# A hybrid decoder layer on one core: first loads in one block, one power for four norms, two turnings of the queue moved, last rows in smaller pieces

## Chip, cores and metric

The kernel runs on 1 core of one Trainium2 chip, in float32. The metric is device time in microseconds (us), the median of several executions; a profile is taken from one execution.

## What is computed

One layer over 512 tokens of width 1024 (reference, cut):

```python
h  = rmsnorm(x, g_mix);  z = h @ w_in           # 1024 x 9728: all projections
rq, rk, rv, rg, aq, ak, av, gl = split(z)
# A: retention, 4 heads, chunks of 128, rotated q and k, decay, group norm, swish gate
# B: 3 groups of 4 heads, dilated causal attention (window, step) = (128,1), (512,4), (2048,16),
#    q and k rms-normed and rotated; the groups merged by their softmax denominators
x  = x + (sig(g_A) * (A @ W_A) + sig(g_B) * (B @ W_B)) @ w_o
x  = x + square(relu(rmsnorm(x) @ w_up)) @ w_down
x  = x + sig(rmsnorm(x) @ w_ple_gate) * (p @ w_ple_proj)
```

## The kernel before

Every large matmul runs in three passes over split operands: each float32 operand is cut into a high part (`hi`) and a low part (`lo`), and `mm3` adds hi*hi, hi*lo and lo*hi. Weights come from HBM in units of 256 rows x 512 columns (512 KB, `raw`), ScalarE (ACT) makes the high part `whi` and VectorE (DVE) the low part `wlo` (`split_unit`, L237 and L238). A plan lists all units in their order; `fetch(n)` issues loads on SyncE's queue (SP) up to unit n, `ahead(n)` splits units ahead of use.

`setup` loads the transposed x (`x_cols`, 8 chunks of 128 rows) and the first panel of `w_in` (group 0's q, 4 units) in alternating transfers of 256 KB on SP; the first chunk of weights comes in two halves of 64 partitions, one on ACT's queue, one on SP's. `first_panel` splits x and weights chunk by chunk in a fixed order and begins with chunk 0: hi*hi, lo*hi, hi*lo for four tiles of 128 tokens (L468, L470, L472), then chunks 1 to 3, then for each token tile chunks 4 to 7. `load_tables` and `fetch(6)` (two more units) follow the first loads, then four tiles of x (512 KB each) whose squares `token_squares` takes.

The q projection of group 0 is not normed at once: the tokens' factors come late. For the first three tiles `consume` only takes sums of squares and rotates. At the last tile it takes the tokens' squares, `token_factors` (power on POOL, L527), then four times `factor` (a DVE instruction and a power of 128x4 on POOL, L613 and L614) and four times `scale` (a DVE multiplication of 128x512, L618). In group 0's q and k ACT and DVE keep the written order (`manual_schedule`); elsewhere a list scheduler orders each engine's instructions by readiness and by their order of emission.

TensorE's order around the small stages comes from a queue: `later(lag, fn)` puts a step behind `lag` ticks, a tick comes after every six large matmuls or so, and at every second tick up to two ready steps are emitted, the first in the list first:

```python
def tick(self):
    self.clock += 1
    if self.clock % self.PACE:
        return
    for _ in range(self.PACE):
        i = next((i for i, (ready, _, _) in enumerate(self.queue) if ready <= self.clock), None)
```

So transposes and attention steps stand between the matmuls of the next projection. `merge` is such a step (12 ticks after the last attention group's projections): it computes the merge weights on DVE into `wide` (cw), turns them on TensorE (pc, L756), copies the result (ct), writes it to DRAM (c_dram) and later reads it back broadcast, one row of 512 per head and group (`load`, cb, first three 4 ticks later), multiplies and adds (`weigh`, first 8 ticks later; each step also issues a load three items on). `heads_T` turns rotated heads (ph, L559): four transposes of 128x128 per head, after `lag` ticks. `ret_proj` projects and rotates the retention keys and calls it with 9; after it follow the projections of v and of the gate, then the retention heads that read the turned keys.

At the end `fin` computes sigmoid (ACT), product and sum (DVE) of an output tile and stores it; the last token tile of the second half is made in two column halves of 256.

Of the kernel before, what the change touches and what calls it, by code (L numbers as in the profile page):

```python
# [11 lines left out]
F32 = mybir.dt.float32  # L12
# [64 lines left out]
class Block:  # L77
# [299 lines left out]
    def setup(self):  # L377
        nc, a = self.nc, self.a
        self.gcol = self.const.tile([P, 48], F32, name="gcol")
        xr = [self.big("xr") for _ in range(2)]  # L380
        self.x_cols = [xr[k // 4][:, k % 4] for k in range(KD)]
        nc.scalar.dma_start(self.gcol, a["vec_cols"])
        for u in range(KD // 2):
            src, _ = self.plan[u]
            raw = self.wraw.tile([P, 1024], F32, tag="raw", name=self.nm("raw")).rearrange("p (k n) -> p k n", k=2)
            for k in range(2):
                c = slice((2 * u + k) * P, (2 * u + k + 1) * P)
                nc.sync.dma_start(self.x_cols[2 * u + k], a["x_cols"][c])
                w = src[k * P : (k + 1) * P]
                if u or k:  # L390
                    nc.sync.dma_start(raw[:, k], w)
                else:
                    nc.scalar.dma_start(raw[: P // 2, k], w[: P // 2])
                    nc.sync.dma_start(raw[P // 2 :, k], w[P // 2 :])
            self.raws.append((raw, None))
        self.load_tables()
        self.fetch(6)
        self.x_tiles = []
# [181 lines left out]
    def att_proj(self, g, n):  # L580
# [5 lines left out]
        def consume(t, ps):  # L586
# [8 lines left out]
            if not lazy:  # L595
                factor(t)
                if t:
                    scale(t - 1)
                if t == NT - 1:
                    scale(t)  # L600
            elif t == NT - 2:
                self.token_squares(0)
            elif t == NT - 1:
                self.token_squares(2)
                self.token_factors()
                for i in range(NT):
                    factor(i)
                for i in range(NT):
                    scale(i)
# [112 lines left out]
    def merge(self, groups, oh, ol):  # L722
# [30 lines left out]
        for g in range(NG):  # L753
            nc.vector.tensor_copy(wide[:, g * H * NT : (g + 1) * H * NT].rearrange("p (h r) -> p r h", h=H), cs[g])
        ps = self.bank("pc")
        nc.tensor.transpose(ps[: NG * H * NT, :P], wide, self.ident)  # L756
        turned = self.tmp("ct")[: NG * H * NT, :P]
        nc.scalar.activation(turned, ps[: NG * H * NT, :P], AF.Copy)
        cd = self.dram.tile([NG * H, S], F32, name="c_dram", tag="c_dram")
        nc.sync.dma_start(cd.rearrange("a (r l) -> (a r) l", r=DIL), turned)  # L760
        accs, spread = [None] * H, {}
# [22 lines left out]
        for i, (h, g) in enumerate(items):  # L784
            if i == 0:
                for p in items[:3]:
                    self.later(4, lambda p=p: load(*p))

            def step(i=i, h=h, g=g):
                weigh(h, g)  # L790
                if i + 3 < len(items):
                    load(*items[i + 3])
            self.later(8, step, ("O", h, g))


    def ret_proj(self, extra=None):
# [9 lines left out]
        self.rows_gemm(self.hT, KD, consume)  # L806
        return self.heads_T(rots, False, 9)

# [254 lines left out]
    def tail(self, mx):  # L1063
# [85 lines left out]
        for half in range(2):  # L1149
# [3 lines left out]
            def fin(t, ps, i=slice(0, 512)):  # L1153
                s, o = self.tmp("fs"), self.tmp("fo")
                c = slice(half * 512 + i.start, half * 512 + i.stop)
                nc.scalar.activation(s[:, i], ps[:, i], AF.Sigmoid, scale=r3[:, t : t + 1])
                nc.vector.tensor_tensor(o[:, i], s[:, i], pp[half][:, t, i], op=ALU.mult)
                nc.vector.tensor_tensor(s[:, i], o[:, i], xs[t][:, c], op=ALU.add)
                nc.sync.dma_start(out[t * P : (t + 1) * P, c], s[:, i])

# [65 lines left out]
```

## Time and profile before

| | |
|---|---|
| median of 3 runs | 996.74 us (996.7 to 998.17) |
| the profiled execution | 997.21 us, its span 995.4 us |
| TensorE busy | 984.7 us, 99% of the span |
| VectorE, ScalarE, GpSimd busy | 647.6, 461.8, 97.4 us |
| granted TensorE clock | full in all 40 slices |

The span is what the profiler saw from the first to the last instruction; the time also has what lies around it. TensorE's busy time is from modelled ends of matmuls: its matmuls of 512 columns start closer together than the duration shown. What it waits for is read from the rows below.

### The profile page before, as it was taken

How to read it: one execution, taken by the hardware profiler on the slowest of the kernel's cores; microseconds unless marked ns; L12 is line 12 of the kernel's file. 1: busy time of each engine (PE TensorE's matmuls, PEld its weight loads, DVE VectorE, ACT ScalarE, POOL GpSimd, SP SyncE). 2: the span in 40 equal slices, each digit the busy share in tenths (PEclk: the TensorE clock that was granted, in tenths of full speed). 3: DMA queues.
4: the chain of work that ended last, by engine and by line, in shares of the span. 5: the costliest groups of instructions: out<-in, count | busy, mean ns of one | idle time of the engine just before them, and what ended most of it. 6: DMA issues, size and time to landing. Idle time of an engine off the chain costs nothing.

```text
span 995.4 us, 12449 instructions
## 1 busy us (share of the span) xinstructions
PE 984.7 (99%) x4588; PEld 826.1 (83%) x4588; DVE 647.6 (65%) x1014; ACT 461.8 (46%) x938; POOL 97.4 (10%) x98
## 2 busy tenths in 40 slices
PE   8999999999999999999999999999999999999998
PEld 6788899889887888888888878888888888888886
DVE  6866675774878344554643696668667759766953
ACT  5535344433433334342422447764564565465451
POOL 0210220220000010001002010110101001000000
PEclk9999999999999999999999999999999999999999
DMA  9632132323353312222346496758659766875911
GB/s 337 240 101 76 54 106 85 105 76 106 93 142 120 113 43 85 86 85 85 132 146 166 125 233 193 190 128 225 179 136 212 203 167 153 238 160 131 312 54 53
DMA packets 90781, 141.15 MB, mean 142 GB/s; under 512 B 6320, under 2 KB 40416, under 8 KB 90720
## 3 DMA queue, kind: packets, MB, share of 16 engines
q1 hardware_dynamic: 79616, 119.22, 37.5%
q0 software_dynamic: 10880, 20.97, 12.7%
q8 instruction: 36, 0.59, 0.2%
q10 hardware_dynamic: 224, 0.16, 0.1%
q14 instruction: 25, 0.20, 0.1%
HBM read 136.10 MB, written 4.24 MB: 141 GB/s over the span
## 4 chain that ended last, share of the span: by engine, by line
PE 94%; DVE 4%; issue 1%; DMA 0%; ACT 0%; POOL 0%; ACTq 0%; DVEq 0%; POOLq 0%
PE pg L251 25%; PE pg L250 25%; PE pg L249 25%; PE pb L251 3%; PE pb L249 3%; PE pb L250 3%; PE po L700 1%; PE ph L559 1%; PE pt L325 1%; PE sc L677 1%; DVE wlo L238 1%; PE ry L899 1%; PE pe L651 1%; PE kv L887 1%; PE sc L683 1%
## 5 line engine op out<-in xcount | busy, mean ns | idle before, releaser
L238 DVE TENSOR_TENSOR wlo<-raw,whi 128x1024 fp32r<-128x1024 f32 (+1 forms) x166 | 196.8, 1191 | 103.8 <-ACT whi L237 101.8
L237 ACT ACTIVATE whi<-raw 128x1024 fp32r<-128x1024 f32 (+1 forms) x165 | 169.5, 1032 | 195.3 <-PE pg L251 75.4
L249 PE MATMUL pg<-whi,hh 128*128 128x512 f32 x444 | 178.6, 402 | 0.0
L250 PE MATMUL pg<-wlo,hh 128*128 128x512 f32 x444 | 173.6, 391 | 1.0 <-DVE wlo L238 1.0
L251 PE MATMUL pg<-whi,hl 128*128 128x512 f32 x444 | 173.7, 391 | 0.0
L250 PEld LDWEIGHTS pg<-wlo,hh 128*128 128x128 f32 x444 | 91.4, 206 | 15.3 <-DVE wlo L238 1.4
L251 PEld LDWEIGHTS pg<-whi,hl 128*128 128x128 f32 x444 | 91.1, 205 | 15.1
L249 PEld LDWEIGHTS pg<-whi,hh 128*128 128x128 f32 x444 | 91.3, 206 | 14.0
L249 PE MATMUL pg<-h2h,whi 128*128 128x512 f32 x256 | 99.6, 389 | 0.0
L250 PE MATMUL pg<-h2l,whi 128*128 128x512 f32 x256 | 99.6, 389 | 0.0
L251 PE MATMUL pg<-h2h,wlo 128*128 128x512 f32 x256 | 99.6, 389 | 0.0
L242 ACT ACTIVATE whi<-raw,gcol 128x256 fp32r<-128x256 f32 (+1 forms) x144 | 66.1, 523 | 21.3 <-PE pg L250 12.4
L243 DVE SCALAR_TENSOR_TENSOR wlo<-raw,gcol,whi 128x256 fp32r<-128x256 f32 (+1 forms) x144 | 65.5, 510 | 15.6 <-ACT whi L242 15.6
L202 POOL DMA_DIRECT2D raw<-in_w_down x32 | 38.6, 1206 | 302.4 <-DMA raw<-in_w_down 147.8
L249 PE MATMUL pg<-hh,whi 128*128 128x512 f32 x160 | 64.0, 400 | 0.0
L249 PE MATMUL pg<-whi,uh 128*128 128x512 f32 x160 | 62.8, 392 | 0.0
L251 PE MATMUL pg<-whi,ul 128*128 128x512 f32 x160 | 62.6, 392 | 0.0
L250 PE MATMUL pg<-wlo,uh 128*128 128x512 f32 x160 | 62.4, 390 | 0.0
L251 PE MATMUL pg<-hh,wlo 128*128 128x512 f32 x160 | 62.4, 390 | 0.0
L250 PE MATMUL pg<-hl,whi 128*128 128x512 f32 x160 | 62.3, 390 | 0.0
L250 PEld LDWEIGHTS pg<-h2l,whi 128*128 128x128 f32 x256 | 48.0, 188 | 10.0
L251 PEld LDWEIGHTS pg<-h2h,wlo 128*128 128x128 f32 x256 | 48.0, 188 | 10.0
(201 smaller groups left out, 1685.2 us busy)
## 6 DMA issues: line engine op xcount, KB each, us to landing
raw<-in_w_in SPq DMA_DIRECT2D x72, 512.0 KB, 4.1
raw<-in_w_down SPq DMA_DIRECT2D x48, 512.0 KB, 4.3
raw<-in_w_up SPq DMA_DIRECT2D x32, 512.0 KB, 5.2
raw<-in_w_down POOLq DMA_DIRECT2D x32, 512.0 KB, 6.7
raw<-in_w_o SPq DMA_DIRECT2D x12, 512.0 KB, 4.3
x<-in_x SPq DMA_DIRECT2D x8, 512.0 KB, 7.1
raw<-in_w_ret_out SPq DMA_DIRECT2D x8, 512.0 KB, 3.5
raw<-in_w_o POOLq DMA_DIRECT2D x8, 512.0 KB, 5.8
```

Of the source, the lines that this page charges most:

```text
L202: self.nc.gpsimd.dma_start(raw, rows(add[0]), accum_op=ALU.add)
L237: self.pin(nc.scalar.activation(R(hi[:, i]), raw[:, i], AF.Copy))
L238: nc.vector.tensor_tensor(R(lo[:, i]), raw[:, i], hi[:, i], op=ALU.subtract)
L242: self.pin(nc.scalar.activation(R(hi[:, i]), raw[:, i], AF.Copy, scale=g))
L243: nc.vector.scalar_tensor_tensor(R(lo[:, i]), raw[:, i], g, hi[:, i], op0=ALU.mult, op1=ALU.subtract)
L249: t.matmul(ps, sh, mh, start=first, stop=False, skip_group_check=more)
L250: t.matmul(ps, sh, ml, start=False, stop=False, skip_group_check=more)
L251: t.matmul(ps, sl, mh, start=False, stop=last, skip_group_check=more)
L325: nc.tensor.transpose(ps[:, k * P : (k + 1) * P], part[:, k * P : (k + 1) * P], self.ident)
L559: self.nc.tensor.transpose(ps[:, t * P : (t + 1) * P], rots[t][:, h * HD : (h + 1) * HD], self.ident)
L651: self.nc.tensor.transpose(ps[:, k * P : (k + 1) * P], e[:, k * P : (k + 1) * P], self.ident)
L677: nc.tensor.matmul(sc[:, h * P : (h + 1) * P], qT[:, h, rs], kT[:, h, rs], start=True, stop=True)
```

## The change

1. x_cols and the first panel's weights lie side by side in one array `front` (1024 x 1024). Each chunk of 128 rows comes with one transfer of 512 KB on SP into a tile `front`; only chunk 0 comes with two (x, then weights). ACT's queue has no part in it. The units' raw buffers are these tiles, so four buffers of `raw` are free and `fetch(8)` loads four more units instead of two before the x tiles.
2. The four `factor` calls of group 0's q become four DVE instructions into one tile of 128x16 and one power on POOL over it, with -0.5 broadcast.
3. In `merge`, transpose, copy and write of the weights become a step 4 ticks later; the first loads come 6 ticks later instead of 4, the first `weigh` 10 instead of 8.
4. `ret_proj` turns its heads after 14 ticks instead of 9.
5. The last 256 columns of the last token tile are finished in two pieces of 128.

```diff
--- before.py
+++ after.py
@@ -377,24 +377,19 @@
     def setup(self):
         nc, a = self.nc, self.a
         self.gcol = self.const.tile([P, 48], F32, name="gcol")
-        xr = [self.big("xr") for _ in range(2)]
-        self.x_cols = [xr[k // 4][:, k % 4] for k in range(KD)]
         nc.scalar.dma_start(self.gcol, a["vec_cols"])
+        self.x_cols = []
         for u in range(KD // 2):
-            src, _ = self.plan[u]
-            raw = self.wraw.tile([P, 1024], F32, tag="raw", name=self.nm("raw")).rearrange("p (k n) -> p k n", k=2)
+            front = self.big("front")
             for k in range(2):
-                c = slice((2 * u + k) * P, (2 * u + k + 1) * P)
-                nc.sync.dma_start(self.x_cols[2 * u + k], a["x_cols"][c])
-                w = src[k * P : (k + 1) * P]
-                if u or k:
-                    nc.sync.dma_start(raw[:, k], w)
-                else:
-                    nc.scalar.dma_start(raw[: P // 2, k], w[: P // 2])
-                    nc.sync.dma_start(raw[P // 2 :, k], w[P // 2 :])
-            self.raws.append((raw, None))
+                both = front[:, 2 * k : 2 * k + 2]
+                src = a["front"][(2 * u + k) * P : (2 * u + k + 1) * P].rearrange("p (c n) -> p c n", c=2)
+                for c in (0, 1) if u == 0 and k == 0 else (slice(0, 2),):
+                    nc.sync.dma_start(both[:, c], src[:, c])
+                self.x_cols.append(both[:, 0])
+            self.raws.append((front.rearrange("p (k c) n -> p k c n", c=2)[:, :, 1], None))
         self.load_tables()
-        self.fetch(6)
+        self.fetch(8)
         self.x_tiles = []
         xb = [self.big("x") for _ in range(2)]
         for t in range(NT):
@@ -603,8 +598,12 @@
             elif t == NT - 1:
                 self.token_squares(2)
                 self.token_factors()
+                v4, r4 = self.small(NT * H, "v"), self.small(NT * H, "r")
                 for i in range(NT):
-                    factor(i)
+                    c = slice(i * H, (i + 1) * H)
+                    nc.vector.tensor_scalar(v4[:, c], sums[i][0], 1.0 / HD, self.floor[:, i : i + 1], op0=ALU.mult, op1=ALU.add)
+                    sums[i] = None, None, r4[:, c]
+                nc.gpsimd.tensor_tensor(r4, v4, self.mhalf.unsqueeze(1).to_broadcast([P, NT, H]), op=ALU.pow)
                 for i in range(NT):
                     scale(i)
 
@@ -752,12 +751,16 @@
         wide = self.tmp("cw")[:, : NG * H * NT]
         for g in range(NG):
             nc.vector.tensor_copy(wide[:, g * H * NT : (g + 1) * H * NT].rearrange("p (h r) -> p r h", h=H), cs[g])
-        ps = self.bank("pc")
-        nc.tensor.transpose(ps[: NG * H * NT, :P], wide, self.ident)
-        turned = self.tmp("ct")[: NG * H * NT, :P]
-        nc.scalar.activation(turned, ps[: NG * H * NT, :P], AF.Copy)
         cd = self.dram.tile([NG * H, S], F32, name="c_dram", tag="c_dram")
-        nc.sync.dma_start(cd.rearrange("a (r l) -> (a r) l", r=DIL), turned)
+
+        def turn():
+            ps = self.bank("pc")
+            nc.tensor.transpose(ps[: NG * H * NT, :P], wide, self.ident)
+            turned = self.tmp("ct")[: NG * H * NT, :P]
+            nc.scalar.activation(turned, ps[: NG * H * NT, :P], AF.Copy)
+            nc.sync.dma_start(cd.rearrange("a (r l) -> (a r) l", r=DIL), turned)
+
+        self.later(4, turn)
         accs, spread = [None] * H, {}
         nat = lambda ap: ap.rearrange("p (l r) -> p r l", r=DIL)
 
@@ -784,13 +787,13 @@
         for i, (h, g) in enumerate(items):
             if i == 0:
                 for p in items[:3]:
-                    self.later(4, lambda p=p: load(*p))
+                    self.later(6, lambda p=p: load(*p))
 
             def step(i=i, h=h, g=g):
                 weigh(h, g)
                 if i + 3 < len(items):
                     load(*items[i + 3])
-            self.later(8, step, ("O", h, g))
+            self.later(10, step, ("O", h, g))
 
 
     def ret_proj(self, extra=None):
@@ -804,7 +807,7 @@
                 extra(t, rots[t])
 
         self.rows_gemm(self.hT, KD, consume)
-        return self.heads_T(rots, False, 9)
+        return self.heads_T(rots, False, 14)
 
     def ret_cols(self):
 
@@ -1152,11 +1155,14 @@
 
             def fin(t, ps, i=slice(0, 512)):
                 s, o = self.tmp("fs"), self.tmp("fo")
-                c = slice(half * 512 + i.start, half * 512 + i.stop)
-                nc.scalar.activation(s[:, i], ps[:, i], AF.Sigmoid, scale=r3[:, t : t + 1])
-                nc.vector.tensor_tensor(o[:, i], s[:, i], pp[half][:, t, i], op=ALU.mult)
-                nc.vector.tensor_tensor(s[:, i], o[:, i], xs[t][:, c], op=ALU.add)
-                nc.sync.dma_start(out[t * P : (t + 1) * P, c], s[:, i])
+                n = 128 if t == NT - 1 and i.start else i.stop - i.start
+                for b in range(i.start, i.stop, n):
+                    p = slice(b, b + n)
+                    c = slice(half * 512 + b, half * 512 + b + n)
+                    nc.scalar.activation(s[:, p], ps[:, p], AF.Sigmoid, scale=r3[:, t : t + 1])
+                    nc.vector.tensor_tensor(o[:, p], s[:, p], pp[half][:, t, p], op=ALU.mult)
+                    nc.vector.tensor_tensor(s[:, p], o[:, p], xs[t][:, c], op=ALU.add)
+                    nc.sync.dma_start(out[t * P : (t + 1) * P, c], s[:, p])
 
             self.rows_gemm(h3, KD, fin, need=need, group=GG[half], halves=half == 1)
         order.__exit__(None, None, None)
@@ -1209,7 +1215,8 @@
         g = inputs[n][0].reshape(NG, 2, HD // 2)
         qk += [g.reshape(NG, HD), g[:, ::-1].reshape(NG, HD)]
     data["rot_gains"] = np.ascontiguousarray(np.stack(qk, 1).reshape(1, -1))
-    data["x_cols"] = np.ascontiguousarray(inputs["x"][0].T)
+    data["front"] = np.ascontiguousarray(np.concatenate(
+        [inputs["x"][0].T, inputs["w_in"][0][:, AQ : AQ + 512]], 1))
     data["p_cols"] = np.ascontiguousarray(inputs["p"][0, 0].T)
     data["vec_cols"] = np.ascontiguousarray(np.concatenate(
         [inputs[n][0] for n in ("g_mix", "ret_gn", "b_gate", "g_ple", "g_mlp")]).reshape(-1, P).T)
```

## Rows read from the trace of the kernel before

**Rows 1.** The page: what the DMA engines moved in each of 40 slices of the span (24.9 us each), and the chain that ended last, its shares of the span by engine.

```profile
GB/s 337 240 101 76 54 106 85 105 76 106 93 142 120 113 43 85 86 85 85 132 146 166 125 233 193 190 128 225 179 136 212 203 167 153 238 160 131 312 54 53
...
PE 94%; DVE 4%; issue 1%; DMA 0%; ACT 0%; POOL 0%; ACTq 0%; DVEq 0%; POOLq 0%
```

**Rows 2.** The view of waits, TensorE's matmuls alone: who waited for whom, us in total, times, the longest.

```profile
PE pg L468 <- DVE whi L233: 1.9, 1, 1.9
PE warm L411 <- DVE warm L407: 1.5, 1, 1.5
PE ph L559 <- DVE ro L549: 1.2, 1, 1.2
PE pg L250 <- DVE wlo L238: 1.0, 1, 1.0
PE pc L756 <- DVE cw L754: 0.8, 1, 0.8
```

**Rows 3.** The timeline of the first 10 us, all engines: start us, duration us, engine, line, operation, output and inputs, shapes, count, and in brackets the idle time of the engine before it and what ended it. SPq and ACTq are the issues of transfers on the queues of SyncE and ScalarE.

```profile
1.18 0.55 SPq L394 DMA_DIRECT2D raw<-in_w_in  x1
...
1.19 0.55 ACTq L393 DMA_DIRECT2D raw<-in_w_in  x1
...
2.40 0.43 SPq L391 DMA_DIRECT2D raw<-in_w_in  x1
...
5.96 0.43 DVE L233 CAST whi<-raw 128x512 fp32r<-128x512 f32 x1 [4.56 <-DMA raw<-in_w_in]
...
6.44 0.72 ACT L449 ACTIVATE hh<-xr,gcol 128x512 fp32r<-128x512 f32 x1 [1.76 <-DMA xr<-in_x_cols]
...
6.53 1.17 PE L468 MATMUL pg<-whi,hh 128*128 128x512 f32 x4 [1.90 <-DVE whi L233]
...
7.57 0.75 DVE L450 SCALAR_TENSOR_TENSOR hl<-xr,gcol,hh 128x512 fp32r<-128x512 f32 x1
...
8.23 0.68 DVE L238 TENSOR_TENSOR wlo<-raw,whi 128x512 fp32r<-128x512 f32 x1
...
9.58 0.39 PE L250 MATMUL pg<-wlo,hh 128*128 128x512 f32 x1
```

**Rows 4.** The DMA view of the issues from 1.15 to 1.3 us (the first two) and from 2.3 to 2.5 us (the third): queue, count, size, median us from issue to landing.

```profile
raw<-in_w_in SPq DMA_DIRECT2D x1, 128.0 KB, 3.1
...
raw<-in_w_in ACTq DMA_DIRECT2D x1, 128.0 KB, 4.7
...
raw<-in_w_in SPq DMA_DIRECT2D x1, 256.0 KB, 4.7
```

**Rows 5.** The timeline from 33 to 41 us, of POOL, DVE and PE: the norm factors of the first projection, the scales, the next weights' low halves and the matmuls that want them.

```profile
34.81 3.94 POOL L614 TENSOR_TENSOR r<-v,mhalf 128x4 f32<-128x4 f32 x4
...
35.86 0.69 DVE L618 TENSOR_TENSOR ro<-ro,r 128x512 f32<-128x512 f32 x1 [1.17 <-POOL r L614]
...
38.78 0.69 DVE L618 TENSOR_TENSOR ro<-ro,r 128x512 f32<-128x512 f32 x1 [0.28 <-POOL r L614]
...
39.39 4.62 DVE L238 TENSOR_TENSOR wlo<-raw,whi 128x1024 fp32r<-128x1024 f32 x4
...
39.27 0.39 PE L249 MATMUL pg<-whi,hh 128*128 128x512 f32 x1
...
40.66 0.50 PE L250 MATMUL pg<-wlo,hh 128*128 128x512 f32 x1 [1.00 <-DVE wlo L238]
```

**Rows 6.** The timeline of POOL: single powers of 128x4 and of 128x1 at other places (columns as in rows 3).

```profile
46.96 1.01 POOL L614 TENSOR_TENSOR r<-v,mhalf 128x4 f32<-128x4 f32 x1 [8.21 <-DVE v L613]
...
99.54 1.38 POOL L614 TENSOR_TENSOR r<-v,mhalf 128x4 f32<-128x4 f32 x1 [37.99 <-DVE v L613]
...
353.42 0.55 POOL L315 TENSOR_TENSOR r<-v,mhalf 128x1 f32<-128x1 f32 x1 [132.24 <-DVE v L314]
```

**Rows 7.** The issue of the four x tiles in the timeline, the DMA view of the last of them (issued from 14.9 to 15.8 us), and the third of the four squares that read them.

```profile
13.40 2.38 SPq L402 DMA_DIRECT2D x<-in_x  x4
...
x<-in_x SPq DMA_DIRECT2D x2, 512.0 KB, 10.3
...
30.53 1.08 ACT L517 ACTIVATE j<-x 128x1024 f32<-128x1024 f32 x1
```

**Rows 8.** The timeline of PE around the transpose of the merge weights.

```profile
265.21 0.39 PE L251 MATMUL pg<-hh,wlo 128*128 128x512 f32 x1
...
266.37 0.27 PE L756 MATMUL pc<-ident,cw 128*48 128x128 f32 x1 [0.77 <-DVE cw L754]
```

**Rows 9.** The timeline of PE around the transposes of the retention keys: two groups of eight and the matmul after each.

```profile
308.47 0.71 PE L559 MATMUL ph<-ident,ro 128*128 128x128 f32 x5
...
310.68 0.47 PE L249 MATMUL pg<-whi,hh 128*128 128x512 f32 x1
...
313.51 1.03 PE L559 MATMUL ph<-ident,ro 128*128 128x128 f32 x8
...
314.30 0.48 PE L249 MATMUL pg<-whi,hh 128*128 128x512 f32 x1
```

**Rows 10.** The view by stretches: start and end, us, busy time of each engine with its count of instructions (PE, PEld, DVE, ACT, POOL), granted clock, DMA share, GB/s.

```profile
287.00:311.00 24.00, 22.80 (x106) 18.73 (x105) 23.11 (x40) 8.96 (x11) 0.00 (x0) 1.00 0.48 150
```

**Rows 11.** The timeline of the last instructions of ACT and DVE.

```profile
991.10 0.47 ACT L1156 ACTIVATE fs<-pg,r 128x256 f32<-128x256 f32 x1 [2.40 <-PE pg L251]
...
992.07 0.42 DVE L1158 TENSOR_TENSOR fs<-fo,x 128x256 f32<-128x256 f32 x1
```

## The prediction

> **What bounds the kernel now.** I read the chain that ended last first. TensorE holds 94% of it [rows 1], so the time is TensorE's matmul stream plus the places where that stream stands still, and any edit is worth what it takes from those places. The view of TensorE's waits lists them all [rows 2]: 1.9 us before the first real matmul, 1.0 us at a low weight half (wlo), 0.8 us at the merge weights' transpose (pc), 1.2 us at the retention keys' transposes (ph); the 1.5 us of the warm-up matmuls stays. They make 4.9 us of 995.4. Each part of the change but the last aims at one of them, so I price each from the few microseconds around it. Outside the span lie 1.8 us (997.21 against 995.4). A wait counts from a matmul's modelled end, so I take the loss from start to start: 13 intervals lie between 6.53 and 9.58 [rows 3], so a matmul starts every 0.23 us.
>
> **First loads.** Before, the first weight block comes in two halves: the SP half lands at 1.18 + 3.1 = 4.28, the ACT half at 1.19 + 4.7 = 5.93 [rows 3, 4], the cast follows at 5.96 and TensorE starts at 6.53. The change sends the whole block as SP's second transfer. It can't land before 4.28, when only half of it was there, and I put no later end than 5.93. In the old run the x block behind it was done soon after 5.93 (ACT takes it at 6.44 [rows 3]), so much of the time to 5.93 went to that block: I take 5.2, near the middle, and TensorE starts 0.6 later, at 5.8. What is late next is chunk 1. Its x and weights are now one 512 KB transfer, and its x, which landed for 6.44, comes with the weights, which had landed at 2.40 + 4.7 = 7.10 [rows 3, 4] behind the same bytes. From there: hh 0.72, hl, then wlo; hl starts 0.03 after hh ends, wlo starts 0.66 after hl and takes 0.68 [rows 3], so wlo is there at 7.10 + 0.72 + 0.03 + 0.66 + 0.68 = 9.19 and its matmul starts at about 9.24. TensorE would want it at 5.8 + 3.05 = 8.85 and had it at 9.58. **Term: -0.34 us.** Bounds: -1.65 if the block lands at 4.28 and chunk 1 early enough, +0.45 if chunk 1 lands one 256 KB step late (0.26 MB at the 337 GB/s of [rows 1], 0.8 us). Chunks 2 to 7 follow at the loads' pace; the stream takes 12 matmuls, 2.7 us, for each of chunks 1 to 3, so it doesn't meet them. SP issues 9 transfers instead of 16 for these blocks, off the path.
>
> A rule speaks against this edit: the Trainium skill (DMA: Bandwidth & Descriptors, Rules for kernel authors) says that two transfers to disjoint partition halves aren't worth making since both run on the same engines, so joining them would give nothing: the block would land at 5.93, the term would be 0 and the sum 995.1. The trace has the halves 1.65 us apart, which the rule doesn't give.
>
> **Two weight blocks more ahead of x.** fetch(8) puts 1.05 MB before the four x tiles. At 337 GB/s (the first slice [rows 1]) that is 3.1 us. The last x tile was issued before 15.8 and took 10.3 [rows 7]: 26.1 at the latest, then 29.2, for squares that start at 30.53. Cover 1.3 us, 1.0 after the earlier start. **Term: 0.**
>
> **One power for four norms.** POOL runs four powers of 128x4 from 34.81 on; the first scale starts 1.05 later, the last at 38.78, the weight split behind them in DVE's written order at 39.39, and the matmul that wants it at 40.66 [rows 5]. It was due at 39.27 + 0.23 = 39.50. With one power of 128x16 no scale can start before all sixteen are done, and three scales lose the cover of the power beside them. No row shows 128x16. A power of 128x1 takes 0.55 us and one of 128x4 takes 1.01 where DVE works little beside it in the timeline, 1.38 where it works on [rows 6]. DVE waits here, so I take 1.01: (1.01 - 0.55) / 3 = 0.153 us an element, and 1.01 + 12 x 0.153 = 2.85 us for sixteen. First scale: 34.81 + 2.85 + 0.04 = 37.70; four scales at 0.61 (38.78 to 39.39); the split at 40.14 instead of 39.39. **Term: +0.75 us**: the stall grows. Bounds: if a short POOL instruction costs the same whatever its length, 1.05 to the first scale, the split at 38.30 and -1.09; with 1.38 and 0.55 the slope is 0.277, the power 4.70 and the term +2.60. Break-even is a power of 2.1 us. I take the middle value since it is the line through the two rows without a busy DVE.
>
> **Merge weights turned 4 steps later.** The transpose pc was next after the matmul of 265.21, so due at 265.44, and started at 266.37 [rows 8]: 0.93 lost, waiting for DVE's copy cw. Moved four queue steps of six matmuls, 4 x 6 x 0.23 = 5.5 us past its call, it meets a cw long there. **Term: -0.93 us**, bounds -0.93 and 0 (it waits as long in the new place). What moves with it: the copy ct, the write c_dram, the twelve loads cb and weigh steps, each two steps (2.7 us) later in emission, the first chain link ct itself later. SP issues the weights of later panels behind these loads; DVE gets the weigh steps nearer to the retention keys' rotation, where it is busy 23.11 of 24 us [rows 10].
>
> **Retention keys turned at 14 instead of 9.** The eight transposes that start at 308.47 end for the next matmul at 310.68, 2.21 later; the next eight take 314.30 - 313.51 = 0.79 [rows 9]. 1.42 lost, for DVE's last rotation, done at about 310.3 (three of the transposes, 0.1 each, still come before 310.68). The queue is looked at every second step, so five steps are four or six: 4 x 6 x 0.23 = 5.5 us, due at about 313.9, 3.6 after the rotation. The keys' first reader stands behind two passes of 96 matmuls (44 us), so nobody waits for them. **Term: -1.42 us**, bounds -1.42 and 0.
>
> **Last rows.** After the last matmul ACT runs at 991.10 and DVE's second operation of 256 columns, 0.42 long, at 992.07 [rows 11]. In two pieces of 128: one ACT and two DVE instructions and one transfer more. Shorter pieces start DVE about 0.1 earlier, but four DVE operations with their starting costs end about 0.1 later than two; the last transfer is half as long but stands behind one more issue. **Term: 0**, bounds -0.3 and +0.4.
>
> **Sum.** -0.34 + 0.75 - 0.93 - 1.42 = -1.94 us. Against the profiled execution 997.21 - 1.94 = 995.27; that execution is 0.47 above the median, so the median goes from 996.74 to **994.8 us**. The bound of what can be told from no change, 0.2%, is 2.0 us: the forecast lies on its edge.
>
> **Rivals.**
>
> *B, the power is cheap.* The first scale starts at 35.86 as now, the split at 38.30, TensorE at 39.57, and the stall is gone: 1.84 below the forecast, **993.0 us**. For it: the fixed part is most of a 128x1 power. Against it: 128x4 costs nearly double 128x1 [rows 6]. The Trainium skill (GPSIMD Engine Reference, section 3.1) gives some 2.6 cycles an element for a two-input elementwise instruction beyond its dispatch; by that rule twelve elements more cost an estimated 0.03 us, which is this rival. The trace has 0.46 us for three elements and doesn't agree, but a power isn't an add, and the loop may run better at sixteen.
>
> *C, a new wait behind the merge.* The weigh steps of head 0 fall into DVE's full stretch from 287 on, about 4 us of DVE work ahead of the last rotation, against 3.6 us of cover; or a weight block waits on SP behind the cb loads. A stall of the size that was there, 1.2 us: **996.0 us**. For it: 23.11 of 24 us [rows 10]. Against it: as many later weigh steps move behind that rotation.
>
> *D, the power is dear.* DVE's work contends as in the 1.38 row: +1.85 on the forecast, **996.7 us**. Against it: DVE waits for the power.
>
> *E, slower: the x tiles come late.* ACT runs the squares in written order, and behind them stand the norms, the power, the scales and the split for which TensorE waits. Beyond its 1.0 us of cover every microsecond that an x tile is late goes to TensorE. To end slower by 2 us it takes 3.9 us of stall over the forecast, an x tile landing after 34: **998.8 us**. For it: 1.05 MB more in the same queue. Against it: that is 3.1 us, and it would have to be 8.
>
> **How the numbers follow.** Forecast 0.46, B 0.22, C 0.16, D 0.09, E 0.05, and 0.02 for the first loads losing more than I bound. The forecast's own range is 993.5 to 995.6 (the first term's ends), half of its chance on either side of -2.0. Faster by over 0.2%: 0.23 of the forecast, 0.22 of B, 0.02 of C, 0.47. Slower by over 0.2%: 0.06 (E and part of the rest). Within 0.2%: 0.47. The range that leaves out no more than 2 in 10 reaches from B to D: 992.7 to 996.8.
>
> **What the changed profile would show.** TensorE starting at about 5.8 with a wait of some 0.4 for chunk 1's wlo; POOL with one power of some 2.85 us, TensorE's wait for wlo near 39 grown to about 1.8; no wait at pc and none at ph; the last DVE operation ending as far from the last matmul as now (1.4 us). I am wrong if the power's length is far from 2.85, if a wait appears between 260 and 345 that isn't there now, or if the first block lands far from 5.2.

## The result: slower by 0.2%, and the profile after

The changed kernel takes 1000.5 us, the kernel before 998.18 us, medians of 20 runs each; the ratio is 1.0022, 95% interval 1.0016 to 1.0028. The profiled execution of the changed kernel has a span of 998.0 us, against 995.4 before. The median of the three runs of before from which the prediction started (996.74) lies near the quick end of the 20 (996.47 to 1000.57), so 1.4 us of the distance to the forecast 994.8 belong to that base. Two runs of the later series are slow outliers and left out of every ratio and count: one of before (3478 us) and one of all_mended (1237 us).

TensorE's waits after the change, us in total, times, the longest; they answer to [rows 2]:

```profile
PE pg L250 <- DVE wlo L238: 3.0, 2, 2.6
PE warm L406 <- DVE warm L402: 1.5, 1, 1.5
PE pg L249 <- ACT rz L804: 1.1, 1, 1.1
PE pg L249 <- ACT whi L237: 0.6, 1, 0.6
PE pg L463 <- DVE whi L233: 0.4, 1, 0.4
```

The waits at pc and ph are gone and the first one shrank, but the wait for wlo grew to 2.6 us, and a new one stands at rz. To place the difference I lined up the two traces matmul by matmul (the n-th 512-column matmul of one against the n-th of the other). TensorE is 0.14 us behind at 11 us, 3.3 at 47, 2.45 at 280, 2.45 again at 330, 2.2 at the end (0.2 comes back at one place near 602 us). Five stretches hold it. At one of them, the merge weights, the wait is simply gone: from 3.3 to 2.45. The other four follow.

The first loads, in the timeline of the first 10 us, which answers to [rows 3]:

```profile
4.44 0.43 DVE L233 CAST whi<-front 128x512 fp32r<-128x512 f32 x1 [3.03 <-DMA front<-in_front]
5.01 1.29 PE L463 MATMUL pg<-whi,hh 128*128 128x512 f32 x4 [0.38 <-DVE whi L233]
7.42 0.72 ACT L444 ACTIVATE hh<-front,gcol 128x512 fp32r<-128x512 f32 x1 [2.67 <-DMA front<-in_front]
8.72 0.51 PE L249 MATMUL pg<-whi,hh 128*128 128x512 f32 x1 [0.58 <-ACT whi L237]
9.59 0.50 PE L250 MATMUL pg<-wlo,hh 128*128 128x512 f32 x1 [0.36 <-DVE wlo L238]
```

TensorE starts 1.5 us earlier and gives it back: chunk 1, now one transfer, lands for 7.42, TensorE waits twice, and the matmul of its wlo starts at 9.59, where it started at 9.58 before.

The norm factors, in the timeline of POOL and DVE from 31 to 41 us, which answers to [rows 5]:

```profile
32.93 0.69 DVE L568 TENSOR_TENSOR C<-rotc,mg 128x512 f32<-128x512 f32 x1 [0.72 <-DMA mg<-in_rot_gains]
34.15 0.16 DVE L519 TENSOR_SCALAR v<-ss 128x4 f32<-128x4 f32 x1
35.77 2.90 POOL L606 TENSOR_TENSOR r<-v,mhalf 128x16 f32<-128x16 f32 x1
38.71 2.50 DVE L617 TENSOR_TENSOR ro<-ro,r 128x512 f32<-128x512 f32 x4 [3.07 <-POOL r L606]
41.12 4.62 DVE L238 TENSOR_TENSOR wlo<-raw,whi 128x1024 fp32r<-128x1024 f32 x4
```

The power takes 2.90 us. But the whole chain also starts 0.96 later, because DVE's tables for the keys (C, L568), which stand ahead of the factors in DVE's written order, wait for the rotation gains. SyncE issues those at 22.70, at 19.13 before. The weight split comes at 41.12 instead of 39.39, and TensorE waits 2.6 us for it. The issues in SyncE's timeline, before (the first three lines: three weight blocks go ahead of the gains) and after (the last three: six go):

```profile
12.04 1.06 SPq L200 DMA_DIRECT2D raw<-in_w_in  x2
17.71 0.38 SPq L200 DMA_DIRECT2D raw<-in_w_in  x1
19.13 0.33 SPq L432 DMA_DIRECT2D mg<-in_rot_gains  x1
8.69 4.21 SPq L200 DMA_DIRECT2D raw<-in_w_in  x4
18.65 1.75 SPq L200 DMA_DIRECT2D raw<-in_w_in  x2
22.70 0.34 SPq L427 DMA_DIRECT2D mg<-in_rot_gains  x1
```

What follows the stall is in the view by stretches (us, busy time with its count of TensorE's matmuls, PEld, DVE, ACT, POOL, granted clock, DMA share, GB/s):

```profile
42.00:43.00 1.00, 0.60 (x2) 0.54 (x3) 1.00 (x2) 0.00 (x0) 0.00 (x0) 0.91 0.00 0
43.00:44.00 1.00, 1.00 (x4) 0.73 (x3) 1.00 (x2) 0.00 (x0) 0.00 (x0) 0.50 0.00 0
44.00:45.00 1.00, 1.00 (x4) 0.81 (x3) 1.00 (x2) 0.00 (x0) 0.00 (x0) 0.50 0.00 0
45.00:46.00 1.00, 1.00 (x3) 0.77 (x3) 0.75 (x1) 0.00 (x0) 0.00 (x0) 0.50 0.00 0
47.00:48.00 1.00, 1.00 (x7) 0.79 (x5) 0.02 (x1) 0.95 (x8) 0.00 (x0) 1.00 0.53 80
```

After the stall the granted clock is 0.50 (the 1.2 GHz level) for more than 3 us: TensorE is busy all the time, and its matmuls start 0.43 us apart instead of 0.23. From its timeline:

```profile
43.50 0.63 PE L250 MATMUL pg<-wlo,hh 128*128 128x512 f32 x1
43.93 0.63 PE L251 MATMUL pg<-whi,hl 128*128 128x512 f32 x1
```

That costs 1.6 us beside the stall's 1.6 of growth.

The retention keys, in the timeline around 309 us, which answers to [rows 9]:

```profile
307.84 1.14 ACT L783 ACTIVATE oh<-mt 128x512 fp32r<-128x512 f32 x1 [8.14 <-DVE mt L779]
308.78 0.63 ACT L804 ACTIVATE rz<-pg,r 128x512 f32<-128x512 f32 x1
309.47 0.50 PE L249 MATMUL pg<-whi,hh 128*128 128x512 f32 x1 [1.15 <-ACT rz L804]
317.78 1.03 PE L554 MATMUL ph<-ident,ro 128*128 128x128 f32 x8
```

The eight transposes run through. But TensorE now waits 1.15 us for a bank that rz (the copy of the last token tile out of it) must free: rz stands on ACT behind oh, and oh waits 8.14 us for DVE's weigh steps.

Last, the tail: DVE's last operation ends 1.86 us after the last matmul's start (1.71 before), and the span ends 3.2 after that (2.9 before).

### The profile page after: what moved, and what is told of

Its sections match the earlier page's. It is cut to its first block, busy times and chain, and to the rows that moved or that the text cites. A ratio compares the mean times of both kernels' runs of the same rounds, so it can differ in the third digit from the quotient of the medians.

```text
span 998.0 us, 12431 instructions
## 1 busy us (share of the span) xinstructions
PE 986.7 (99%) x4588; PEld 827.4 (83%) x4588; DVE 647.2 (65%) x1016; ACT 461.1 (46%) x939; POOL 96.4 (10%) x95
## 3 DMA queue, kind: packets, MB, share of 16 engines
q0 software_dynamic: 10880, 20.97, 12.6%
## 4 chain that ended last, share of the span: by engine, by line
PE 69%; DVE 0%; ACT 0%; issue 0%
PE pg L251 19%; PE pg L249 19%; PE pg L250 19%; PE pb L251 3%; PE pb L249 3%; PE pb L250 3%; PE pt L325 1%; PE ry L902 1%; PE kv L890 1%; PE ry L904 1%; PE pa L251 0%; PE pa L249 0%; PE pa L250 0%; PE rs L882 0%; PE pb L325 0%; PE ph L554 0%
## 5 line engine op out<-in xcount | busy, mean ns | idle before, releaser
L238 DVE TENSOR_TENSOR wlo<-raw,whi 128x1024 fp32r<-128x1024 f32 (+1 forms) x158 | 191.2, 1216 | 102.6 <-ACT whi L237 100.7
L237 ACT ACTIVATE whi<-raw 128x1024 fp32r<-128x1024 f32 (+1 forms) x158 | 165.1, 1049 | 194.1 <-PE pg L251 74.3
L249 PEld LDWEIGHTS pg<-h2h,whi 128*128 128x128 f32 x256 | 48.1, 188 | 9.9
```

The source lines that it names most:

```text
L237: self.pin(nc.scalar.activation(R(hi[:, i]), raw[:, i], AF.Copy))
L238: nc.vector.tensor_tensor(R(lo[:, i]), raw[:, i], hi[:, i], op=ALU.subtract)
L249: t.matmul(ps, sh, mh, start=first, stop=False, skip_group_check=more)
```

## The experiments

Kernels with a single time were run once and are read from their traces, against the profiled execution of before; "TensorE's position" is the shift of its matmuls against that execution.

**The gains' wait: is it fetch(8)?**

```
-        self.fetch(8)
+        self.fetch(6)
```

> The changed kernel with fetch(6) instead of fetch(8): only two further weight blocks go ahead of the x tiles, as before the change. Theory S (the stall's parts add up, and TensorE's clock falls because the stall gets too long): DVE's table product no longer waits 0.7 us for the gains, TensorE's stall near 39 us shrinks from 2.8 to about 1.9 us, the granted clock stays at 1.0 behind it, and the span goes from 998.0 to about 995.6 (0.8 of the gains' wait and 1.6 of the slow clock). Rival C (the half clock belongs to that place or to the earlier start, not to the stall's length): the stall shrinks too but the clock still falls, span about 997.2.

1000.73 us. The gains are issued at 23.30, DVE's tables still wait 0.74, the stall is 2.6 and the clock falls. The two blocks ahead of x are not the cause.

**Four powers.**

```
-                v4, r4 = self.small(NT * H, "v"), self.small(NT * H, "r")
...
+                for i in range(NT):
+                    factor(i)
```

> The changed kernel with the four powers of 128x4 back, each followed by nothing but its scale as before. Theory S: the stall near 39 us shrinks by 0.77 to about 2.0 us, the clock stays at 1.0, span about 995.6. Rival C: the stall shrinks, the clock still falls to half for some 3 us, span about 997.2. If the one power were no loss at all the stall would stay at 2.8.

999.2 us. The four powers are back at 3.94 us in all, but the tables wait 1.32 for the gains, TensorE still waits 2.4, and the clock falls to half. The execution is not quite like the changed kernel's: TensorE stands 0.46 earlier in it (-0.32 against +0.14), and the tables start at 33.07 instead of 32.93, so the chain behind the gains is 0.6 later for TensorE. Without that I estimate the stall at 1.8: the four powers do give back their 0.8.

**Merge at once** (pc, the loads cb and the weigh steps as before).

```
-        self.later(4, turn)
...
-                    self.later(6, lambda p=p: load(*p))
+                    self.later(4, lambda p=p: load(*p))
...
-            self.later(10, step, ("O", h, g))
+            self.later(8, step, ("O", h, g))
```

> The changed kernel with the merge's turning back in its old place and its loads and weigh steps at 4 and 8 ticks. Theory M (the later weigh steps made ACT's copy rz wait, and TensorE for it): the wait at pc of about 0.8 to 0.9 us is back, the wait of 1.15 us for rz at 309.5 is gone, keys turned without a wait; span about 997.6. Rival K (the keys' later turning made the rz wait): both waits stand, span about 998.9.

1000.53 us. The wait at pc is back (1.05), the wait for rz is gone, and none stands at ph. So it is the later steps of the merge that make rz late; weigh_later, below, narrows it to the loads and weigh steps.

**Keys at 9 again.**

```
-        return self.heads_T(rots, False, 14)
+        return self.heads_T(rots, False, 9)
```

> The changed kernel with the retention keys turned after 9 ticks again. Theory M: the wait for rz stays at about 1.1 us and a wait at the keys' transposes comes on top, up to 1.4 us: span 998.0 to 999.4. Rival K: the wait for rz goes and the old wait at the keys' transposes comes back: span about 998.1 with no rz wait in TensorE's list.

999.96 us. The rz wait stays at 1.17 and there is none at ph: once rz stops TensorE for that long, the transposes come late enough with either lag. What TensorE loses at these places together, from start to start as in the prediction: 2.35 before, 1.21 with the keys' edit alone (merge_at_once), 1.32 with the merge's alone (this run), 1.31 with both. The two gains don't add.

**Gains first** (the gains move from behind the mask to behind the x tiles), and the same with four powers:

```
             self.x_tiles.append(v)
+        self.gain_rows(1, NG)
...
-        self.gain_rows(1, NG)
```

> The gains of the later groups are issued right behind the x tiles, ahead of the mask and of the weight blocks that now go before them; all else as in the changed kernel. Theory G (the gains' lateness is one of two causes of the longer stall): DVE's tables of group 1 wait for no transfer, v stands near 33.2 instead of 34.15, the first scale near 37.8, the low weight half near 40.2, and TensorE loses 1.8 to 2.0 us near 39 instead of 2.6. Then the granted clock says which of two: if it stays at full speed the span falls by 0.8 + 1.6 = 2.4 us to some 995.6; if it still falls to half for some 3 us, by 0.8 to some 997.2. Rival (DVE's tables wait for something else, or the factors for the squares of x): v stays near 34.1 and the stall at 2.6.

997.79 us, span 995.9. The tables don't wait, TensorE waits 1.78, and its position goes from +0.40 to +1.18 over the stall. The granted clock stays at 1.00.

> The same, with the four powers back. If the stall is a sum of the gains' wait and of the power's length, both are now gone: the first scale 1.05 after v, TensorE loses 1.0 to 1.3 us near 39 as before the change, the granted clock stays at full speed there, and the span is 2.6 - 1.2 = 1.4 us of stall and 1.6 us of clock shorter than the changed kernel's, some 995.0. If the clock fell for a reason other than the stall's length (the earlier start of the loads, say), it still falls near 43 and the span is some 996.6.

997.84 us, span 996.1. TensorE waits 1.0 and its position is +0.87 before and after: nothing lost against before. Between the two kernels lies the power alone: 0.78 us.

**Gains first, split first:** the two weight blocks are split behind the one power's issue, ahead of the scales.

```
                 nc.gpsimd.tensor_tensor(r4, v4, self.mhalf.unsqueeze(1).to_broadcast([P, NT, H]), op=ALU.pow)
+                self.ahead(4)
```

> One power of sixteen as in the changed kernel, gains first, and the two weight blocks that stood behind the scales in DVE's written order are split while POOL works on the power. If DVE's written order is what turns the power's 2.9 us into a stall, TensorE waits less than 0.3 us between 36 and 44, its clock stays at full speed, and the span falls by 2.6 + 1.6 = 4.2 us to some 993.8. If the next thing TensorE wants there (the scaled queries' transposes) is as late as the split was, a wait of 1 us or more stands at those transposes instead and the span is some 995 to 996.

996.54 us, span 994.7. From the timelines of DVE and POOL:

```profile
35.92 2.35 DVE L238 TENSOR_TENSOR wlo<-raw,whi 128x1024 fp32r<-128x1024 f32 x2
36.14 4.90 POOL L606 TENSOR_TENSOR r<-v,mhalf 128x16 f32<-128x16 f32 x1
41.07 2.50 DVE L618 TENSOR_TENSOR ro<-ro,r 128x512 f32<-128x512 f32 x4 [2.80 <-POOL r L606]
```

DVE splits while POOL works, scales 5 us later than before, and TensorE doesn't stop at all: its position falls by 1.3 us over the place. The scales were never wanted that early. The power itself takes 4.90 us with DVE's two splits beside it, against 2.90; here nobody waits for those 2 us.

**Weigh later.**

```
-                    self.later(6, lambda p=p: load(*p))
+                    self.later(20, lambda p=p: load(*p))
...
-            self.later(10, step, ("O", h, g))
+            self.later(24, step, ("O", h, g))
```

> The changed kernel with the twelve loads of merge weights 14 queue steps later and the weigh steps 14 steps later, behind the last rotation of the retention keys. If the 1.15 us wait for rz at 309.5 comes from the weigh steps of head 0 standing ahead of it (oh waits 8 us for DVE, and rz stands behind oh on ACT), the wait goes, no wait at ph takes its place, and the span falls by 1.3 us to some 996.7. If it comes from elsewhere (the rotation itself), it stays and the span is some 998. If the later loads meet the weight blocks on SP, a new wait for a weight half stands between 300 and 345.

999.68 us. No wait at rz, ph or pc: TensorE's position falls by 0.90 at pc and by 1.45 between 293 and 337 us, and stays. Both predicted gains are real once the weigh steps stand behind the last rotation. (The total is high for the other reason: the gains came 1.57 late here, and the stall with half speed behind it took TensorE's position from +0.1 to +3.9.)

**First loads undone** (the setup lines and fetch(6) of the kernel before), the rest as changed.

> The first loads and the six blocks ahead of x as before, everything else as in the changed kernel. Theory R (the gains are late because the joined loads leave six raw buffers free, so that more weight blocks go ahead of the gains): DVE's tables wait for no transfer, TensorE starts at 6.5, loses 1.8 to 1.9 us near 40 (1.0 plus 0.8 for the power), its clock stays at full speed, 0.9 us come back at the merge weights and nothing net at the keys: span 995.4 + 0.8 - 0.9 + 0.4 for the last rows = 995.7. Rival (the gains are late for another reason): the stall is 2.4 us or more, the clock falls to half for some 3 us, span some 997.5 or more.

1000.92 us, span 999.1. Half a miss: the gains are issued at 19.27 and don't make DVE wait, TensorE waits 1.78, as theory R says. But the clock falls all the same, only later than in the changed kernel (so the earlier start of the loads isn't what makes it fall); and the first matmuls run at half speed, which puts TensorE 1.85 us back by 11 us.

```profile
43.00:44.00 1.00, 0.71 (x3) 0.61 (x4) 1.00 (x2) 0.00 (x0) 0.00 (x0) 1.00 0.00 0
45.00:46.00 1.00, 1.00 (x3) 0.74 (x3) 1.00 (x2) 0.00 (x0) 0.00 (x0) 0.50 0.00 0
47.00:48.00 1.00, 1.00 (x4) 0.81 (x3) 0.00 (x0) 0.88 (x7) 0.00 (x0) 0.50 0.15 38
```

So the same wait of 1.78 us was followed by half speed here and not in gains_first. That was still open, and three kernels with one part of the change each were timed, each against before (medians of 12 runs; before 998.8 beside them).

**Power alone** (of the diff only the six lines of the power, in the kernel before).

> The kernel before with the one power of sixteen and nothing else changed. The stall near 40 grows by 0.78 us as in the two kernels that showed it. If the clock stays at full speed after a stall of that length, the medians differ by 0.8 (ratio 1.0008). If it falls in most executions, as in loads_undone, they differ by up to 2.4 (ratio 1.0024); in about half of them, by some 1.6.

1000.6 us, ratio 1.0019 (1.0010 to 1.0028): the one power alone is about as much slower as the whole change.

```profile
42.00:43.00 1.00, 0.00 (x0) 1.00 0.00 0
44.00:45.00 1.00, 1.00 (x4) 0.58 0.00 0
45.00:46.00 1.00, 1.00 (x3) 0.50 0.00 0
46.00:47.00 1.00, 1.00 (x4) 0.50 0.00 0
```

(TensorE alone: busy, granted clock, DMA share, GB/s.) The stall is the same 1.78, and the clock falls behind it.

**Loads alone** (only the setup lines, fetch(8) and the array front).

> The kernel before with the joined first loads and the eight blocks ahead of x, all else as before. DVE's tables wait 0.7 to 1.3 us for the gains and the stall near 40 grows by about that. If that decides, the kernel is slower by 1 us, and by up to 2.6 where the clock falls (ratio 1.001 to 1.0026). If the earlier start (TensorE at 5.0 to 5.6 instead of 6.3 to 6.5) decides, it is level or up to 1 us faster (0.999 to 1.0).

999.2 us, ratio 1.0016 (1.0003 to 1.0028). In its profile TensorE's position was +0.74 at 11 us, so late that the gains were there in time; the clock stayed. So the loads alone are slower too, if barely, and the parts' ratios don't add to that of the whole.

**Turns alone** (only turn, the lags 6 and 10 and the lag 14).

> The kernel before with the later turns of merge weights and keys, all else as before. If the rz wait eats the keys' gain, only the merge weights' 0.9 us is left: ratio 0.999. If the two gains add after all, 2.3 us: ratio 0.9977.

998.31 us, ratio 0.9998 (0.9988 to 1.0008). Its profile has no wait at pc and ph and 1.16 us at rz: 0.9 us gained. The timing can't tell it from nothing.

Each timed run also has a mean granted clock. Runs with 0.998 or less: before 7 of 51, turns_alone none of 12, loads_alone 5 of 12, power_alone 9 of 12, the changed kernel 18 of 20. In power_alone those 9 take 1000.9 us on average, the other 3 take 999.0; in the changed kernel 1000.6 against 998.7. The mean doesn't say where in a run the clock fell, and it is no clean sign: one run in 11 of all_mended (below) has 0.998 too, a kernel whose profile has no such stall, and in before the 7 runs take only 0.4 us more than the others. The profiles say where: up to the last matmul the clock falls nowhere but behind this stall. It doesn't fall in the four whose stall is 1.0 to 1.1 us, it falls in two of the three with 1.78 and in all six with 2.4 or more. I read it as: the longer the stall, the more often the clock falls, at about 1.9 us a fall.

**The change mended.** Four kernels with the split first, weigh steps later and keys at 14. With the first loads as before and the last rows whole:

> The first loads as before, one power with the two weight blocks split while POOL works on it, merge weights turned 4 steps later and weighed behind the keys' last rotation (loads 14 and weigh steps 14 steps later than in the changed kernel), keys at 14, last rows whole. If each wait has the cause that I give it, none is left but the start: span 995.4 - 1.0 (split) - 0.9 (merge weights) - 1.4 (keys) = 992.0, ratio to before 0.9966. If the waits replace one another as in the changed kernel, a new one stands at the scaled queries' transposes or behind the weigh steps after 310, and the span is 993 or more.

995.79 us, ratio 0.9974 (0.9963 to 0.9985). No wait of TensorE is left but those at the start; span 993.6. It misses 992.0 mostly by what the start loses (+1.38 at 11 us).

> The kernel all_mended with the last rows in pieces of 128 columns as in the changed kernel. If the pieces cost what they seemed to cost there, the time from the last matmul to the end is 0.4 us longer than in all_mended, and the medians differ by 0.2 to 0.5. If that was an accident of one execution, they differ by less than 0.2.

995.55 us, ratio 0.9975 (0.9966 to 0.9984). The pieces of 128 make no difference that can be measured: DVE ends 1.86 after the last matmul's start instead of 1.70, and the span ends 3.1 after that instead of 3.4.

With the joined loads, gains behind the x tiles, and chunk 1's x and weights as two transfers:

```
-                for c in (0, 1) if u == 0 and k == 0 else (slice(0, 2),):
+                for c in (0, 1) if u == 0 else (slice(0, 2),):
```

> The kernel all_mended, but with the joined first loads, eight blocks ahead of x, the gains behind the x tiles, and chunk 1's x and weights as two transfers. If the joined loads are worth their earlier start, chunk 1's matmuls run on at 8.1 without a wait and TensorE is up to 1.0 us ahead of before at 11 us: span 991.0 to 992.0. If the first matmuls run at half speed as in several of the runs so far, the start is lost again: TensorE at 11 us is between 0.4 ahead and 1.3 behind before, and the kernel is no faster than all_mended.

**992.91 us, ratio 0.9948 (0.9935 to 0.9962): about 0.5% faster than the kernel before** (six runs; the changed kernel's 1000.5 is from another series). Its waits:

```profile
PE warm L407 <- DVE warm L403: 1.5, 1, 1.5
PE pg L463 <- DVE whi L233: 0.3, 1, 0.3
PE pg L250 <- DVE wlo L238: 0.2, 1, 0.2
```

> The kernel joined_loads_mended with chunk 1's x and weights in one transfer, as in the changed kernel. If the two transfers of chunk 1 make its start even, TensorE waits about 1 us for chunk 1 again and the median is 0.7 to 1.0 us above 992.9. If the start varies whatever the transfers are, its runs spread over 2 us, as those of all_mended do, with a median some 1.3 higher.

994.15 us, ratio 0.9957 (0.9945 to 0.9970). The median is 1.2 us later without chunk 1's two transfers, and the six runs spread over 1.9 us, with them over 0.8. The two kernels were timed in different series, though: against before in its own series the difference is 0.9, and the two intervals overlap, so that the two transfers help is likely and not shown. Neither expectation was quite it: a later median and a wider spread both came.

## Why the prediction was wrong, step by step

By the profiled executions, measured against forecast: the start +0.14 (-0.34), the stall +3.2 (+0.75), the merge weights -0.9 (-0.93), the keys 0 (-1.42), the end +0.4 (0); with the 0.2 at 602 us that is +2.6 in place of -1.94. Of the signs of being wrong that the prediction named, two came: a wait between 260 and 345 us that was not there before (rz), and a first block far from 5.2.

**The stall near 40 us is the step that failed**, by 2.4 us. The power's own term was right: 2.90 us against the 2.85 worked out from two rows, and +0.78 against +0.75 on TensorE. Two things were missing.

- *The gains.* I priced fetch(8) by the x tiles alone and asked only which wait ended last before. The joined blocks live in buffers of their own, so the six raw buffers are free, and six further weight blocks go ahead of the gains, where three went before. That, not fetch(8), is shown by two_blocks_ahead (late with fetch(6)) and loads_undone (in time with the old loads). It cost 0.8 (2.6 us against 1.78 in gains_first).
- *The clock.* I had the stall growing from 1.0 to 1.8 us and took a stall to cost its length. It costs its length and, in most executions, 1.6 to 1.9 us more at half speed behind it. Nothing in the profile of before shows this, since its clock stood at 1.00 throughout; but by the counts above, unsure as they are, it falls in some 7 of 51 runs of before. The Trainium skill (TensorE: Matmul & The Clock Gate, Part 1: The HAM clock gate) has a gate between the two levels, 1.2 and 2.4 GHz; I weighed no rule of it in the prediction and gave the case no chance. The rows from 43 to 46 us agree with that page: matmuls 0.43 us apart, against 0.23 elsewhere.

**First loads.** TensorE does start earlier, at 5.01 where 5.8 was forecast, but the gain was lost in the start itself. The block landed for 4.44 (bounds 4.28 and 5.93, taken 5.2), wlo of chunk 1 was done at 9.53 against the 9.19 worked out, since chunk 1 landed 0.3 late. (The 0.03 between hh and hl in that sum isn't in [rows 3], where 0.41 lies between them; it measured 0.04.) The reference was off too: in before's profiled execution the first matmuls run at full speed. In the five other profiles with the old loads they don't, and TensorE is at 11 us 1.4 to 2.8 later than there; with the joined loads and chunk 1 in one piece -0.3 to 1.4 later (eleven profiles). Much of that is when the clock rises in an execution (last section) and not the loads. Where it rises between 9.3 and 10.9 us, TensorE is on average 1.6 behind with the old loads (four profiles) and 1.0 with the joined ones (six); where it rises by 5.3 us, before stands at 0 and the joined loads at 0.0 to 0.4 (four). So the profiles have the joined loads worth some 0.6 us in the one case and nothing in the other. The timed medians of all_mended and mended_chunk1_joined, which differ in the loads and in the gains' place, lie 1.6 us apart, in different series. The Trainium skill (DMA: Bandwidth & Descriptors, Rules for kernel authors) says that two transfers to disjoint partition halves aren't worth making. I had read from it that joining them gives nothing and the block lands at 5.93, which doesn't follow: it came 1.5 us earlier in one piece, and the page's advice, one transfer, agrees with that. The page also says that such halves serialize, so that they landed 1.65 us apart isn't against it.

**Merge weights:** -0.90 against -0.93, right.

**Keys**, the second step that failed: the wait at ph went (-1.42), as forecast, and rival C took its place: the weigh steps in DVE's full stretch. I had priced C at 1.2 and looked for it at the last rotation; it came at rz, through ACT's order: oh waits for DVE, and rz stands behind oh. What failed is "as many later weigh steps move behind that rotation". weigh_later shows that the term was there to be had.

**Two blocks ahead of x:** 0, right. **Last rows:** 0, right; the profiled +0.4 lies at the bound, and the timed pair shows none of it.

Of the rivals, B fell (128x16 costs 2.90, not the 1.0 that B needs). D's price did not come in the changed kernel, where DVE waits for the power; but D was right that DVE's work makes the power dear: with the split first it takes 4.90 us, near the 4.70 of that bound. E's x tiles came in time (the third square starts at 30.67, with TensorE's own shift of 0.14); but E's end, behind the norms, was the right place with the wrong transfer.

What stays open: why one and the same stall is followed by half speed in one execution and not in another. The runs give the shares, not the reason. Open too is what the joined loads are worth at the start, between nothing and 1.6 us.

## What to carry to other kernels

Where an edit frees buffers, list every transfer that may now go ahead of others in the same queue, and look at the readers of each, also those that have no wait today. Before a stall is priced by its length, ask what TensorE's clock does behind it; a stall that can be filled by moving other work of the same engine ahead (the split ahead of the scales) cost nothing at all here. Two gains that lie behind each other on one engine's queue don't add unless the work that is pushed along leaves that stretch.

## What the runs showed of the hardware

A power of 128x16 on POOL takes 2.90 us, so the line through 128x1 (0.55) and 128x4 (1.01) holds: some 0.15 us an element. That is so in all eight profiles in which DVE waits for it (2.90 or 2.91). In all five in which DVE splits two weight blocks beside it the same power takes 4.90 or 4.91, while DVE's split keeps its 1.2 us a block.

At the start the matmuls can run at half speed while the view by stretches prints a granted clock of 1.00. From the timeline and the view by stretches of gains_first_split_first:

```profile
5.23 2.05 PE L463 MATMUL pg<-whi,hh 128*128 128x512 f32 x4 [0.60 <-DVE whi L233]
7.07 1.91 PE L465 MATMUL pg<-whi,hl 128*128 128x512 f32 x4
8.78 1.91 PE L467 MATMUL pg<-wlo,hh 128*128 128x512 f32 x4
8.00:9.00 1.00, 1.00 (x4) 1.00 0.98 401
```

Four matmuls take 1.7 to 1.8 us from start to start, in the changed kernel 0.9. The 1.00 isn't a measurement there: the trace's own list of clock stretches, from which the views are made, begins with a stretch at full clock at 10.81 us in this execution, and where nothing is listed the view prints 1.00. The list begins at 4.82 us in before, at 5.27 in the changed kernel, and between 4.4 and 12.6 over all eighteen profiles; in the twelve in which it begins after 7 us the slow matmuls end within 0.2 us of that time. Together with what the loads do, this moves TensorE by up to 2.8 us at 11 us. The Trainium skill (TensorE: Matmul & The Clock Gate, Part 1: The HAM clock gate) says that the count of slow matmuls at a start differs from run to run of one kernel. Here it differs from none in before to 14 in turns_alone, but each of these is one execution of another kernel, so no run here shows it for one kernel alone.
